# Gate projections of the DeltaNet branch between the branch products of the merge, and sums of the middle branches on VectorE alone

## The chip, the cores and the metric

One core of a Trainium2 chip runs the whole program in one launch. The core has five engines that run side by side, each with its own instruction stream in a fixed order: TensorE (PE, matrix products, with its weight loads shown as PEld), VectorE (DVE), ScalarE (ACT), GpSimd (POOL) and SyncE (SP, which here only issues DMAs). They wait for each other by semaphores. The metric is the time of one execution in microseconds of device time, as the median of several runs; less is better.

## The reference

The program computes one layer of a streaming encoder for two groups of tokens (1024 prompt tokens and 64 sample tokens with a cache of 256; 1088 columns in all), in float32, with width 1024. What matters here is the mixing step:

```
proj = u @ w_in                                  # u = rms_norm(x), 1088 x 1024
fox, dif, sb, gdn, gates = split(proj)           # gates: 4 branches x 1024 columns
o_fox  = softmax attention with a forget bias    # 4 heads of 64, causal
o_diff = rms_norm(softmax(q1 k1) v - lam * softmax(q2 k2) v)   # chunk-causal
o_sb   = stick-breaking attention                # strictly causal
o_gdn  = gated DeltaNet: short convolution, chunks of 64, a recurrence over chunks
gate   = sigmoid(gates)                          # per branch, 1088 x 1024
merged = sum over b of gate[b] * (o_b @ w_branch[b])           # o_b is 1088 x 256
x = x + merged @ w_out
x = x + (silu(h @ wg) * (h @ wu)) @ wd           # h = rms_norm(x)
y = rms_norm(x)
```

The caches' new rows, the DeltaNet state and the convolution state are outputs too.

## The kernel before, in words

**Numbers.** Each float32 operand of a large product is split into two float16 parts, high and low, and a product is three matmuls into one PSUM bank: high x high, high x low, low x high. `gemm_a` (lines 176 to 187) does that with the weights as the stationary operand: for each of `K` blocks of 128 rows it issues three matmuls with up to 364 columns. A split of weights is one ScalarE copy with scale (`acopy`, line 61) and one VectorE instruction that takes the remainder (`stt`, line 64); `load_unit` does it for a unit of 1024 x 256 weights, in two halves of 512 KB.

**Gate projections.** `spill_gates(b, sp)` is a generator that computes the gate logits of one branch: 4 units of weights, each 2 x 128 output rows x 3 pieces of 364, 364 and 360 columns, 24 groups in all. A group is 24 matmuls (8 blocks x 3) into one of two PSUM banks of tag `d`, a ScalarE copy into a tile `ths` of two buffers, and a store to DRAM (`gtd[b]`) issued from GpSimd's queue; then it yields. The four generators are put on the list `dense` before the forgetting attention begins, in the order sb, fox, diff, gdn.

**Order of the work.** A scheduler at build time simulates the engines and puts each engine's instructions into a fixed order: an instruction written earlier goes first if it is ready, and one written later may go ahead of it into a hole. Three things steer it. `fill(us)` inside the attention loops takes groups from `dense` until their stated costs (3.7 each) use up the given allowance, which sets where they stand in the written order. `tc.high_priority()` lets loads and evacuations of PSUM go ahead. `tc.issue_after(ins)` forbids the instructions traced inside it to go ahead of `ins` on its engine. What `fill` leaves is run off by `drain(dense)` after `attend_diff`, as written; the scheduler may pull it ahead.

**Attention.** `attend_diff` runs over 2 pairs of heads; in each over the nine query tiles in the order `QORD` = 7, 6, 5, 4, 3, 2, 8, 1, 0 (tile t has (t+1) x 128 keys, tile 8 has 320); in each over 2 heads and 2 halves of a head. For each half `scores` puts the scores into PSUM (tag `s`, three banks), VectorE takes the maximum (line 644), ScalarE the exponential with its sum (line 653); then VectorE combines the halves, ScalarE and VectorE split the result, a transposing DMA turns it, and `diff_out` multiplies with the values.

**Merge.** After the attention a loop runs over the branches in the order sb, fox, diff, gdn (`bi` 0 to 3). It loads and splits the branch's weights (`wb`, tiles `wbh`, `wbl`), loads its outputs `oT`, and makes 24 branch products: 8 blocks of 128 output rows (`d`) x 3 pieces. For each: load the gate logits back (`thg`, line 1137), ScalarE tanh, 6 matmuls into a bank `ptb` taken in turn from the five banks of tags `s` and `g`, one VectorE instruction (1 + tanh) x product, and for all but the first branch an addition to the running sum `mg[d]`. In fox and diff this addition is on VectorE for the third piece and on GpSimd otherwise; in gdn on VectorE for `d % 3 == 2` and on GpSimd otherwise. In gdn the sum is then split into `mT`, the input of the product with `w_out`. `mT` takes the buffer of `u1`, the input of the gate projections, so it can be written only when the last of these is done. Tiles of `th` have 4 buffers in the sb branch and 12 after. Sums `mg0` to `mg2` and the sb branch's `th` lie in the pool `brp`, which is open before `attend_diff` ends; the others in one that opens after it.

`load_out(c)` loads and splits one of four units of `w_out`. It takes its tiles from `wt`, which hands out two slots of the ordinary weight pool and, once `w3` is open, every third time a slot of that pool; `w3` opens after the attention's pool has closed. Units 1 and 2 are loaded in the fox branch, 3 and 0 in the diff branch. The products with `w_out` (`out_tile`, `out_sample`) may not go ahead of the last branch product (`last_ptb`). The second half of the layer follows.

Of the kernel before, what the change touches and what calls it, by code (L numbers as in the profile page):

```python
# [17 lines left out]
P = 128  # L18
# [35 lines left out]
def tile_hybrid_encoder(ctx, tc, i, o):  # L54
# [397 lines left out]
    def scores(ps, n, w, q0, q1, kk, col, mask, diag):  # L452

        two = q1 is not None
        last = mask is None and not two
        pe.matmul(ps[:n, :w], lhsT=q0, rhs=kk[:, col:col + w], start=True, stop=last)
        if mask is not None:
            pe.matmul(ps[:n, diag:diag + n], lhsT=identb[:n, :n], rhs=mask[:n, :n], start=False, stop=not two)
        if two:
            pe.matmul(ps[:n, :w], lhsT=q1, rhs=kk[:, col:col + w], start=False, stop=True)  # L460

    def pv_pair(b, pair, t, n, vt, vl, pts):
        ps = pso("pv")
# [161 lines left out]
    def attend_diff():  # L625
        for pair in range(2):
            kT, vt = load_kv("diff", pair)
            for t in QORD:
                n, kc, W, vl = qgeom(t)
                nb = len(vl)  # L630
                o32 = at.tile([P, 2, 64], F32, tag="o32", name="o32", bufs=3)
                qt = load_q("diff", pair, t, n)
                for hp in range(2):
                    sm = at.tile([P, 16], F32, tag="sm16", name="sm16", bufs=4)
                    pr = []
                    ch = chunks(W)
                    for c in range(2):
                        p = at.tile([P, 1024], F32, tag="wk", name="p", bufs=6)
                        pss = []
                        for cc, (c0, w) in enumerate(ch):  # L640
                            ps = psc()
                            m = mk_diff if (t < 8 and c0 + w == W) else None
                            scores(ps, n, w, qt[:, 2 * hp + c, :n], None, kT[2 * hp + c], kc + c0, m, W - n - c0)
                            vec.tensor_reduce(out=sm[:n, 2 * c + cc:2 * c + cc + 1], in_=ps[:n, :w], op=ALU.max, axis=AX.X)
                            pss.append(ps)
                        nm = sm[:n, 4 + c:5 + c]
                        if len(ch) == 2:
                            tt(nm, sm[:n, 2 * c:2 * c + 1], sm[:n, 2 * c + 1:2 * c + 2], ALU.max)
                            ts(nm, nm, -SC, None, ALU.mult)
                        else:  # L650
                            ts(nm, sm[:n, 2 * c:2 * c + 1], -SC, None, ALU.mult)
                        for cc, (c0, w) in enumerate(ch):
                            act.activation(p[:n, c0:c0 + w], pss[cc][:n, :w], AF.Exp, scale=SC, bias=nm,
                                           accum_out=sm[:n, 6 + 2 * c + cc:7 + 2 * c + cc])
                        if len(ch) == 2:
                            tt(sm[:n, 10 + c:11 + c], sm[:n, 6 + 2 * c:7 + 2 * c], sm[:n, 7 + 2 * c:8 + 2 * c], ALU.add)
                            l = 10 + c
                        else:
                            l = 6 + 2 * c
                        pr.append((p, sm[:n, l:l + 1]))  # L660
                    (p1, l1), (p2, l2) = pr
                    cf, r1 = sm[:n, 12:13], sm[:n, 13:14]
                    vec.reciprocal(cf, l2)
                    stt(cf, cf, l1, nlam[:n], ALU.mult, ALU.mult)
                    vec.reciprocal(r1, l1)
                    ts(r1, r1, PS, None, ALU.mult)
                    stt(p1[:n, :W], p2[:n, :W], cf, p1[:n, :W], ALU.mult, ALU.add)
                    sv, tr = p_tiles(W, n)
                    acopy(sv[:n, 0, :W], p1[:n, :W], r1)
                    stt(sv[:n, 1, :W], p1[:n, :W], r1, sv[:n, 0, :W], ALU.mult, ALU.subtract)  # L670
                    pt = tr()
                    fill(FILL_DIFF * W / 2)
                    diff_out(pair, t, n, nb, vl, vt, hp, pt, o32)
# [360 lines left out]

    bidx = {"fox": 0, "diff": 1, "sb": 2, "gdn": 3}

    def spill_gates(b, sp):
        j = bidx[b]
        for d2 in range(4):
            wu = load_unit([(w_in, 0, OFF_GATE + j * D + d2 * BW, BW)], BW)  # L1040
            for m in range(2):
                d = 2 * d2 + m
                for off, n in PIECES:
                    pg = pd("pgs")
                    gemm_a(pg, wu, m * P, uh, ul, off, n, KD)
                    th = sp.tile([P, 364], F32, tag="ths", name="ths", bufs=2)
                    with tc.high_priority():
                        acopy(th[:, :n], pg[:, :n], 0.5 * IWS)
                    gps.dma_start(gtd[b][d * P:(d + 1) * P, off:off + n], th[:, :n])
                    yield 3.7  # L1050
# [28 lines left out]
    cb = cb_.enter_context(tc.tile_pool(name="cb", bufs=1, side="right", reuse_waits="tile"))  # L1079
    gd_ = ExitStack()  # L1080
    g3 = gd_.enter_context(tc.tile_pool(name="gp3", bufs=1, side="right", reuse_waits="tile"))
    dense += [spill_gates(b, sp) for b in gtd]
    side.append(gdn_seq(g3))
    attend_fox()
    drain(side)
# [5 lines left out]
    drain(dense)  # L1091
    ap_.close()
    gp_ = ExitStack()
    mT = up.tile([P, 2, KD, T], F16, tag="u", name="mT")
    w3p = ctx.enter_context(tc.tile_pool(name="w3", bufs=1, reuse_waits="tile"))
    w3.append(w3p)
    w_out = i["w_out"][0]
# [13 lines left out]
    nb_ = [0]  # L1111
    mg = [(brp if d < 3 else gt_pool).tile([P, T], F32, tag=f"mg{d}", name=f"mg{d}") for d in range(KD)]
    order = ("sb", "fox", "diff", "gdn")
    for bi, b in enumerate(order):
        j = bidx[b]
        oT = brp.tile([P, 2, 2, T], F16, tag="oT", name="oT", bufs=2)
        if b in ("sb", "fox"):
            for pr in range(2):
# [9 lines left out]
            acopy(wbh[:, k], wv, WS)  # L1128
            stt(wbl[:, k], wv, WS, wbh[:, k], ALU.mult, ALU.subtract)
        last = bi == len(order) - 1  # L1130
        for c in {1: (1, 2), 2: (3, 0)}.get(bi, ()):
            load_out(c)
        for d, (off, n) in [(d, PIECES[p]) for p in (0, 2, 1) for d in range(KD)] if last else \
                [(d, p) for d in range(KD) for p in PIECES]:
# [3 lines left out]
            act.activation(th[:, :n], th[:, :n], AF.Tanh)  # L1138
            pt = pbk[nb_[0] % len(pbk)]("ptb")
            nb_[0] += 1  # L1140
            last_ptb = gemm_a(pt, (wbh, wbl), d * P, oT[:, 0], oT[:, 1], off, n, 2)
            if bi == 0:
                stt(mg[d][:, off:off + n], th[:, :n], 1.0, pt[:, :n], ALU.add, ALU.mult)
            else:
                stt(th[:, :n], th[:, :n], 1.0, pt[:, :n], ALU.add, ALU.mult)
                tt(mg[d][:, off:off + n], mg[d][:, off:off + n], th[:, :n], ALU.add,
                   eng=vec if (d % 3 == 2 if last else off >= 728) else gps)
            if last:
                sl = slice(off, off + n)
                acopy(mT[:, 0, d, sl], mg[d][:, sl], 0.5 * IWS)  # L1150
# [62 lines left out]
    def out_tile(t, c, wu):  # L1213
        n = rows(t)
        ps = pob[nb_[0] % len(pob)]("pout")
        nb_[0] += 1
        with tc.issue_after(last_ptb.ins):
            gemm_b(ps, n, mT[:, 0], mT[:, 1], t * P, wu, BW)
        cs = slice(c * BW, (c + 1) * BW)
        stt(x2[t][:n, cs], ps[:n, :BW], IWS, x2[t][:n, cs], ALU.mult, ALU.add)  # L1220
# [6 lines left out]
    def out_sample():  # L1227

        for (ca, wa_), (cb2, wb_) in (wus[0:2], wus[2:4]):
            ps = pob[nb_[0] % len(pob)]("pout")  # L1230
            nb_[0] += 1
            with tc.issue_after(last_ptb.ins):
                gemm_2(ps, SMP, mT[:, 0], mT[:, 1], 8 * P, wa_, wb_, BW)
            for r, c in ((slice(0, SMP), ca), (slice(SMP, P), cb2)):
                cs = slice(c * BW, (c + 1) * BW)
# [267 lines left out]
```

## Time and profile before

| what | value |
| --- | --- |
| time of three runs | 1860.31 us median (1857.23 to 1861.63) |
| the profiled execution's own time | 1859.53 us |
| its span, first to last instruction | 1857.4 us |
| TensorE busy | 1730.3 us, 93% |
| VectorE busy | 1252.1 us, 67% |
| ScalarE busy | 863.9 us, 47% |
| GpSimd busy | 301.2 us, 16% |
| TensorE's mean granted clock | 0.981 of full speed |

Times inside the program are microseconds from the start of the span. Busy shares count overlapping instructions of an engine once; a matmul is shown longer than the distance to the next one, because matmuls are pipelined, so the pace is read from the starts. A clock of 1.00 means 2.4 GHz; the other level is 1.2 GHz, and a value between is a mean over time. The releaser of an idle time is inferred from semaphores. The first output of the forgetting attention is stored at 546 us, the first of the differential attention at 699 and its last at 979; the last matmul of a branch product starts at 1077.8 us.

### The profile page before, as it was taken

How to read it: one execution, taken by the hardware profiler on the slowest of the kernel's cores; microseconds unless marked ns; L12 is line 12 of the kernel's file. 1: busy time of each engine (PE TensorE's matmuls, PEld its weight loads, DVE VectorE, ACT ScalarE, POOL GpSimd, SP SyncE). 2: the span in 40 equal slices, each digit the busy share in tenths (PEclk: the TensorE clock that was granted, in tenths of full speed). 3: DMA queues.
4: the chain of work that ended last, by engine and by line, in shares of the span. 5: the costliest groups of instructions: out<-in, count | busy, mean ns of one | idle time of the engine just before them, and what ended most of it. 6: DMA issues, size and time to landing. Idle time of an engine off the chain costs nothing.

```text
span 1857.4 us, 36710 instructions
## 1 busy us (share of the span) xinstructions
PE 1730.3 (93%) x14364; PEld 1226.1 (66%) x14364; DVE 1252.1 (67%) x2589; ACT 863.9 (47%) x1819; POOL 301.2 (16%) x445
## 2 busy tenths in 40 slices
PE   7999983898989899999998899999999999999997
PEld 5678873675655566666665578777758668577573
DVE  7558872997775677786766886758537456465465
ACT  6336551887764555565555533423314223133132
POOL 2114231002212122232133630000000000000002
PEclk9999997999998999999999999999999999999999
DMA  6267798889998975656759846412211113112113
GB/s 225 49 106 212 205 226 137 196 200 213 197 186 202 192 173 141 151 139 172 188 110 283 231 137 109 101 52 69 69 35 58 46 46 91 35 35 69 35 46 102
DMA packets 412158, 244.61 MB, mean 132 GB/s; under 512 B 266146, under 2 KB 389502, under 8 KB 411916
## 3 DMA queue, kind: packets, MB, share of 16 engines
q1 hardware_dynamic: 398944, 205.67, 46.3%
q0 software_dynamic: 13040, 36.60, 7.3%
q8 instruction: 112, 1.84, 0.4%
q14 instruction: 62, 0.51, 0.1%
HBM read 123.39 MB, written 60.81 MB: 99 GB/s over the span
## 4 chain that ended last, share of the span: by engine, by line
PE 42%; DVE 5%; DMA 4%; issue 1%; ACT 1%; POOL 1%; SPq 0%; DVEq 0%; POOLq 0%; ACTq 0%
PE po L1425 12%; PE pb L1309 3%; PE pb L1308 3%; PE pb L1310 3%; PE pc L1309 2%; PE pc L1310 2%; PE pa L1310 2%; PE pc L1308 2%; PE pa L1309 2%; PE pa L1308 2%; PE pout L165 1%; PE pout L166 1%; PE pout L167 1%; PE pgs L184 1%; PE pgs L185 1%
## 5 line engine op out<-in xcount | busy, mean ns | idle before, releaser
L183 PE MATMUL pgs<-u,wh 128*128 128x364 f16 (+1 forms) x768 | 246.3, 321 | 0.0
L185 PE MATMUL pgs<-u,wl 128*128 128x364 f16 (+1 forms) x768 | 246.3, 321 | 0.0
L184 PE MATMUL pgs<-u,wh 128*128 128x364 f16 (+1 forms) x768 | 246.1, 320 | 0.0
L1425 PE MATMUL po<-wh,hT 128*128 128x512 f16 (+1 forms) x792 | 238.1, 380 | 0.6 <-DVE x2a L64 0.6
L1425 PEld LDWEIGHTS <-hT 128*128 128x128 f16 (+1 forms) x1188 | 109.2, 99 | 120.0 <-issue 7.6
L64 DVE SCALAR_TENSOR_TENSOR x2a<-po,x2a 128x512 f32<-128x512 f32 x108 | 74.4, 689 | 140.4 <-PE po L1425 140.2
L61 ACT ACTIVATE wh<-w32f 128x1024 f16<-128x1024 f32 (+1 forms) x90 | 80.3, 926 | 160.2 <-PE po L1425 111.7
L165 PE MATMUL pd<-wh,u 128*128 128x256 f16 (+1 forms) x456 | 126.7, 278 | 29.7 <-DVE qs L64 29.0
L1308 PE MATMUL pb<-X,wh 128*128 128x288 f16 (+1 forms) x528 | 147.1, 279 | 2.5 <-DMA X<-nsh 2.2
L64 DVE SCALAR_TENSOR_TENSOR wl<-w32f,wh 128x1024 f16<-128x1024 f32 (+1 forms) x90 | 94.7, 1065 | 79.5 <-ACT wh L61 79.5
L1309 PE MATMUL pb<-X,wh 128*128 128x288 f16 (+1 forms) x528 | 147.2, 279 | 0.2 <-DMA X<-nsl 0.2
L1310 PE MATMUL pb<-X,wl 128*128 128x256 f16 (+1 forms) x528 | 146.3, 279 | 0.0
L1425 PE MATMUL po<-wl,hT 128*128 128x512 f16 (+1 forms) x396 | 142.0, 379 | 0.0
L1308 PEld LDWEIGHTS <-wh 128*128 128x128 f16 x1232 | 120.5, 98 | 31.0 <-issue 2.4
L1309 PEld LDWEIGHTS <-wh 128*128 128x128 f16 x1232 | 120.5, 98 | 29.9 <-issue 2.4
L1310 PEld LDWEIGHTS <-wl 128*128 128x128 f16 x1232 | 120.5, 98 | 27.2 <-issue 0.8
L166 PE MATMUL pd<-wl,u 128*128 128x256 f16 (+1 forms) x456 | 126.5, 277 | 0.0
L167 PE MATMUL pd<-wh,u 128*128 128x256 f16 (+1 forms) x456 | 126.4, 277 | 0.0
L185 PEld LDWEIGHTS <-wl 128*128 128x128 f16 x912 | 90.0, 99 | 50.9 <-issue 1.5
L183 PEld LDWEIGHTS <-wh 128*128 128x128 f16 x912 | 89.9, 99 | 50.5 <-issue 1.2
L184 PEld LDWEIGHTS <-wh 128*128 128x128 f16 x912 | 89.9, 99 | 49.7 <-issue 0.6
L71 POOL TENSOR_SCALAR fss<-fss 128x1 f32<-128x1 f32 (+1 forms) x9 | 2.0, 220 | 660.3 <-ACT fsq L1454 660.3
(393 smaller groups left out, 4624.6 us busy)
## 6 DMA issues: line engine op xcount, KB each, us to landing
w<-in_w_in_dram SPq DMA_DIRECT2D x56, 512.0 KB, 5.2
w32f<-in_w_ffn_gate_dram SPq DMA_DIRECT2D x20, 512.0 KB, 4.9
w32f<-in_w_ffn_up_dram SPq DMA_DIRECT2D x20, 512.0 KB, 4.0
w32f<-in_w_ffn_down_dram SPq DMA_DIRECT2D x20, 512.0 KB, 3.6
xt<-in_x_prompt_dram SPq DMA_DIRECT2D x8, 512.0 KB, 7.1
wb<-in_w_branch_dram SPq DMA_DIRECT2D x8, 512.0 KB, 4.1
w<-in_w_out_dram SPq DMA_DIRECT2D x8, 512.0 KB, 5.8
x2a<-in_x_prompt_dram SPq DMA_DIRECT2D x8, 512.0 KB, 7.3
```

The source lines that it names most:

```text
L61: return act.activation(out, in_, AF.Copy, scale=scale)
L64: return vec.scalar_tensor_tensor(out=out, in0=in0, scalar=s, in1=in1, op0=op0, op1=op1)
L165: pe.matmul(ps[:n, :N], lhsT=a, rhs=wh[:, k, :N], start=(k == 0), stop=False)
L166: pe.matmul(ps[:n, :N], lhsT=a, rhs=wl[:, k, :N], start=False, stop=False)
L167: pe.matmul(ps[:n, :N], lhsT=b, rhs=wh[:, k, :N], start=False, stop=(k == K - 1))
L183: pe.matmul(ps[:, :n], lhsT=a, rhs=xh[:, k, off:off + n], start=(k == 0), stop=False)
L184: pe.matmul(ps[:, :n], lhsT=a, rhs=xl[:, k, off:off + n], start=False, stop=False)
L185: mm = pe.matmul(ps[:, :n], lhsT=b, rhs=xh[:, k, off:off + n], start=False, stop=(k == K - 1))
L1308: pe.matmul(ps[:, :n], lhsT=wh[:, k], rhs=xh_, start=(start and k == 0), stop=False, skip_group_check=not start)
L1309: pe.matmul(ps[:, :n], lhsT=wh[:, k], rhs=xl_, start=False, stop=False, skip_group_check=not start)
L1310: mm = pe.matmul(ps[:, :n], lhsT=wl[:, k], rhs=xh_, start=False, stop=(k == 3), skip_group_check=not start)
L1425: pe.matmul(ps[h * n:h * n + n], lhsT=hts[k + h][:, a, tk:tk + n], rhs=w[:, k + h], start=(k == 0 and a == 0 and w is wh), stop=(k + nh >= ...
```

## The change

Four things, all in the same place of the program:

1. gdn's gate generator is no longer on `dense`. It is named `late`, and the merge loop asks it for one group after every second branch product of the sb, fox and diff branches (until its 24 groups are used up), and for what is left before the gdn branch. Each group's matmuls may not go ahead of `gate_mark`, which is the last score matmul of pair 1, tile t=3, in `attend_diff`.
2. `mT` is allocated when the generator is done.
3. The additions of the fox and diff branches are all on VectorE. Those of the gdn branch stay as they were.
4. `load_out` of units 1 and 2 moves from the fox to the diff branch, that of 3 and 0 from the diff to the gdn branch.

```diff
@@ -453,11 +453,12 @@
 
         two = q1 is not None
         last = mask is None and not two
-        pe.matmul(ps[:n, :w], lhsT=q0, rhs=kk[:, col:col + w], start=True, stop=last)
+        mm = pe.matmul(ps[:n, :w], lhsT=q0, rhs=kk[:, col:col + w], start=True, stop=last)
         if mask is not None:
             pe.matmul(ps[:n, diag:diag + n], lhsT=identb[:n, :n], rhs=mask[:n, :n], start=False, stop=not two)
         if two:
             pe.matmul(ps[:n, :w], lhsT=q1, rhs=kk[:, col:col + w], start=False, stop=True)
+        return mm
 
     def pv_pair(b, pair, t, n, vt, vl, pts):
         ps = pso("pv")
@@ -640,7 +641,9 @@
                         for cc, (c0, w) in enumerate(ch):
                             ps = psc()
                             m = mk_diff if (t < 8 and c0 + w == W) else None
-                            scores(ps, n, w, qt[:, 2 * hp + c, :n], None, kT[2 * hp + c], kc + c0, m, W - n - c0)
+                            mm = scores(ps, n, w, qt[:, 2 * hp + c, :n], None, kT[2 * hp + c], kc + c0, m, W - n - c0)
+                            if pair == 1 and t == 3:
+                                gate_mark[0] = mm
                             vec.tensor_reduce(out=sm[:n, 2 * c + cc:2 * c + cc + 1], in_=ps[:n, :w], op=ALU.max, axis=AX.X)
                             pss.append(ps)
                         nm = sm[:n, 4 + c:5 + c]
@@ -1034,6 +1037,8 @@
 
     bidx = {"fox": 0, "diff": 1, "sb": 2, "gdn": 3}
 
+    gate_mark = [None]
+
     def spill_gates(b, sp):
         j = bidx[b]
         for d2 in range(4):
@@ -1042,7 +1047,8 @@
                 d = 2 * d2 + m
                 for off, n in PIECES:
                     pg = pd("pgs")
-                    gemm_a(pg, wu, m * P, uh, ul, off, n, KD)
+                    with tc.issue_after(gate_mark[0].ins) if b == "gdn" else ExitStack():
+                        gemm_a(pg, wu, m * P, uh, ul, off, n, KD)
                     th = sp.tile([P, 364], F32, tag="ths", name="ths", bufs=2)
                     with tc.high_priority():
                         acopy(th[:, :n], pg[:, :n], 0.5 * IWS)
@@ -1079,7 +1085,7 @@
     cb = cb_.enter_context(tc.tile_pool(name="cb", bufs=1, side="right", reuse_waits="tile"))
     gd_ = ExitStack()
     g3 = gd_.enter_context(tc.tile_pool(name="gp3", bufs=1, side="right", reuse_waits="tile"))
-    dense += [spill_gates(b, sp) for b in gtd]
+    dense += [spill_gates(b, sp) for b in ("sb", "fox", "diff")]
     side.append(gdn_seq(g3))
     attend_fox()
     drain(side)
@@ -1091,7 +1097,6 @@
     drain(dense)
     ap_.close()
     gp_ = ExitStack()
-    mT = up.tile([P, 2, KD, T], F16, tag="u", name="mT")
     w3p = ctx.enter_context(tc.tile_pool(name="w3", bufs=1, reuse_waits="tile"))
     w3.append(w3p)
     w_out = i["w_out"][0]
@@ -1111,8 +1116,14 @@
     nb_ = [0]
     mg = [(brp if d < 3 else gt_pool).tile([P, T], F32, tag=f"mg{d}", name=f"mg{d}") for d in range(KD)]
     order = ("sb", "fox", "diff", "gdn")
+    late = spill_gates("gdn", sp)
+    ptb = []
     for bi, b in enumerate(order):
         j = bidx[b]
+        if bi == len(order) - 1:
+            for _ in late:
+                pass
+            mT = up.tile([P, 2, KD, T], F16, tag="u", name="mT")
         oT = brp.tile([P, 2, 2, T], F16, tag="oT", name="oT", bufs=2)
         if b in ("sb", "fox"):
             for pr in range(2):
@@ -1128,7 +1139,7 @@
             acopy(wbh[:, k], wv, WS)
             stt(wbl[:, k], wv, WS, wbh[:, k], ALU.mult, ALU.subtract)
         last = bi == len(order) - 1
-        for c in {1: (1, 2), 2: (3, 0)}.get(bi, ()):
+        for c in {2: (1, 2), 3: (3, 0)}.get(bi, ()):
             load_out(c)
         for d, (off, n) in [(d, PIECES[p]) for p in (0, 2, 1) for d in range(KD)] if last else \
                 [(d, p) for d in range(KD) for p in PIECES]:
@@ -1138,13 +1149,15 @@
             act.activation(th[:, :n], th[:, :n], AF.Tanh)
             pt = pbk[nb_[0] % len(pbk)]("ptb")
             nb_[0] += 1
-            last_ptb = gemm_a(pt, (wbh, wbl), d * P, oT[:, 0], oT[:, 1], off, n, 2)
+            ptb.append(gemm_a(pt, (wbh, wbl), d * P, oT[:, 0], oT[:, 1], off, n, 2))
+            if len(ptb) % 2 == 0 and not last:
+                next(late, None)
             if bi == 0:
                 stt(mg[d][:, off:off + n], th[:, :n], 1.0, pt[:, :n], ALU.add, ALU.mult)
             else:
                 stt(th[:, :n], th[:, :n], 1.0, pt[:, :n], ALU.add, ALU.mult)
                 tt(mg[d][:, off:off + n], mg[d][:, off:off + n], th[:, :n], ALU.add,
-                   eng=vec if (d % 3 == 2 if last else off >= 728) else gps)
+                   eng=gps if last and d % 3 != 2 else vec)
             if last:
                 sl = slice(off, off + n)
                 acopy(mT[:, 0, d, sl], mg[d][:, sl], 0.5 * IWS)
@@ -1214,7 +1227,7 @@
         n = rows(t)
         ps = pob[nb_[0] % len(pob)]("pout")
         nb_[0] += 1
-        with tc.issue_after(last_ptb.ins):
+        with tc.issue_after(ptb[-1].ins):
             gemm_b(ps, n, mT[:, 0], mT[:, 1], t * P, wu, BW)
         cs = slice(c * BW, (c + 1) * BW)
         stt(x2[t][:n, cs], ps[:n, :BW], IWS, x2[t][:n, cs], ALU.mult, ALU.add)
@@ -1229,7 +1242,7 @@
         for (ca, wa_), (cb2, wb_) in (wus[0:2], wus[2:4]):
             ps = pob[nb_[0] % len(pob)]("pout")
             nb_[0] += 1
-            with tc.issue_after(last_ptb.ins):
+            with tc.issue_after(ptb[-1].ins):
                 gemm_2(ps, SMP, mT[:, 0], mT[:, 1], 8 * P, wa_, wb_, BW)
             for r, c in ((slice(0, SMP), ca), (slice(SMP, P), cb2)):
                 cs = slice(c * BW, (c + 1) * BW)
```

## Rows read from the trace of the kernel before

**Rows 1.** The page, part 1: busy us (share of the span) xinstructions.

```profile
PE 1730.3 (93%) x14364; PEld 1226.1 (66%) x14364; DVE 1252.1 (67%) x2589; ACT 863.9 (47%) x1819; POOL 301.2 (16%) x445
```

**Rows 2.** Busy time by stretch; after the engines: granted clock, DMA share, GB/s.

```profile
864.00:916.00 52.00, 50.47 (x372) 32.51 (x370) 31.90 (x90) 29.16 (x71) 15.26 (x26) 1.00 0.80 212
916.00:970.00 54.00, 52.62 (x388) 33.70 (x387) 37.77 (x138) 30.06 (x88) 15.08 (x27) 1.00 0.60 142
970.00:1000.00 30.00, 25.70 (x154) 15.25 (x153) 18.43 (x33) 19.80 (x39) 4.71 (x6) 0.94 0.80 240
1000.00:1022.00 22.00, 19.52 (x125) 12.17 (x125) 17.32 (x33) 9.66 (x19) 14.14 (x13) 1.00 0.94 287
1022.00:1046.00 24.00, 20.77 (x132) 12.62 (x131) 22.10 (x33) 12.90 (x26) 17.94 (x19) 1.00 1.05 298
1046.00:1079.00 33.00, 25.94 (x173) 15.79 (x173) 29.37 (x48) 18.97 (x41) 20.40 (x19) 1.00 0.45 134
```

**Rows 3.** Waits of TensorE, 970 to 1079 us: total us, times, longest.

```profile
PE ptb L183 <- DVE thg L64: 13.7, 15, 2.0
PE ptb L183 <- DVE mg L64: 3.3, 4, 2.0
```

**Rows 4.** Tiles gtd_diff, gtd_gdn: ns min/median/max, first and last start us.

```profile
L1049 POOL DMA_DIRECT2D gtd_diff<-ths x24: 539/556/623, 742.3 to 864.6; - x24
...
L1049 POOL DMA_DIRECT2D gtd_gdn<-ths x24: 539/556/626, 868.0 to 973.1; - x24
L1137 SPq DMA_DIRECT2D thg<-gtd_gdn x24: 319/320/1073, 1041.9 to 1068.3; - x24
```

**Rows 5.** Timeline of TensorE at the marked score: start us, duration us.

```profile
916.27 0.38 PE L456 MATMUL psc<-kT,qt 128*128 128x512 f16 x1
```

**Rows 6.** Busy time by stretch, instructions of tile pgs alone.

```profile
864.00:916.00 52.00, 47.01 (x289) 5.36 (x12) 1.00 0.80 212
916.00:970.00 54.00, 46.10 (x280) 5.59 (x12) 1.00 0.60 142
```

**Rows 7.** Timeline of TensorE, gate matmuls and the first sb product.

```profile
902.77 0.32 PE L184 MATMUL pgs<-u,wh 128*128 128x364 f16 x1
...
904.00 0.32 PE L183 MATMUL ptb<-oT,wbh 128*128 128x364 f16 x1
```

**Rows 8.** VectorE by form, 864 to 916: busy us, mean ns, idle before.

```profile
L64 DVE SCALAR_TENSOR_TENSOR wl<-w,wh 128x1024 f16<-128x1024 f32 x4 | 4.8, 1219 | 0.0
L64 DVE SCALAR_TENSOR_TENSOR wbl<-wb,wbh 128x1024 f16<-128x1024 f32 x3 | 3.7, 1226 | 4.8 <-ACT wbh L61 4.8
L67 DVE TENSOR_TENSOR sm<-sm 128x1 f32<-128x1 f32 x16 | 2.5, 154 | 6.9 <-ACT p L653 6.8
```

**Rows 9.** Busy time by stretch, instructions of tile ptb alone.

```profile
864.00:916.00 52.00, 0.63 (x3) 0.00 (x0) 1.00 0.80 212
916.00:970.00 54.00, 3.21 (x18) 1.03 (x2) 1.00 0.60 142
```

**Rows 10.** Tile mg: ns min/median/max, first and last start us.

```profile
L67 DVE TENSOR_TENSOR mg<-mg,thg x22: 519/532/3069, 1002.1 to 1083.3; 128x360 f32<-128x360 f32 x18, 128x364 f32<-128x364 f32 x4
```

**Rows 11.** VectorE by form, 970 to 1079.

```profile
L67 DVE TENSOR_TENSOR mg<-mg,thg 128x360 f32<-128x360 f32 x18 | 16.1, 898 | 0.3
```

**Rows 12.** Timeline of VectorE in the fox branch.

```profile
1002.06 0.52 DVE L67 TENSOR_TENSOR mg<-mg,thg 128x360 f32<-128x360 f32 x1
1002.50 0.52 DVE L64 SCALAR_TENSOR_TENSOR thg<-thg,ptb 128x364 f32<-128x364 f32 x1
```

**Rows 13.** Timeline of the diff branch, VectorE and GpSimd.

```profile
1030.49 4.59 POOL L67 TENSOR_TENSOR mg<-mg,thg 128x364 f32<-128x364 f32 x5
...
1032.42 3.07 DVE L67 TENSOR_TENSOR mg<-mg,thg 128x360 f32<-128x360 f32 x1
```

**Rows 14.** Timeline of TensorE after a wait.

```profile
980.90 0.51 PE L184 MATMUL ptb<-oT,wbh 128*128 128x364 f16 x1
981.20 0.51 PE L185 MATMUL ptb<-oT,wbl 128*128 128x364 f16 x1
```

## Prediction

> **What bounds the kernel now.** I read the busy shares first, then the engines by stretch, then the gate projections by stretch, then the waits of TensorE. [rows 1] shows TensorE busy 93% of the span and VectorE 67%; the program is bound by the order of work on TensorE, and a gain can only come out of TensorE's idle time. [rows 2] shows where that is around the change. From 864 to 970 us TensorE is nearly full: 1.5 and 1.4 us are idle in the first two stretches. In the merge it is not: 4.3 us (970 to 1000, mostly the sb branch), 2.5 us (1000 to 1022, fox), 3.2 us (1022 to 1046, diff), 7.1 us (1046 to 1079, gdn), together 17.1 us. [rows 3] names what ends these waits: in all 19 of them, 17.0 us, a branch product waits for VectorE to empty a PSUM bank.
>
> [rows 4] says what keeps TensorE full before the merge. Gate projections are pulled ahead of their place in the program into every hole of the attention: the last gate tile that is not gdn's leaves for DRAM at 864.6 us, gdn's from 868.0 to 973.1. The tile that `gate_mark` names (pair 1, t=3, last score) runs at 916.3 us [rows 5]. So gdn's gates now begin 52 us ahead of the mark, inside the differential attention. [rows 6] counts them: 289 gate matmuls between 864 and 916, or 12 of gdn's 24 groups, and 280 more up to 970.
>
> **Part 1: gdn's gates may not run before the mark.** The first 72 groups (sb, fox, diff) keep their order, priority and weights, so I take everything up to 864 as unchanged. After that TensorE has no gate work until the mark. Gate matmuls follow each other 0.154 us apart ([rows 7]: eight steps from 902.77 to 904.00), so what leaves the stretch 864 to 916 is 289 x 0.154 = 44.5 us. Of its 50.5 us of TensorE work 6.0 us stay: scores and value products of four tiles.
>
> How short does that stretch get? It cannot shrink to 6 us, for the attention also needs VectorE and ScalarE, which were hidden beside the gates. VectorE works 31.9 us in it [rows 2]. Of this the splits of gate and branch weights take 4.8 + 3.7 us [rows 8], which could run at another time; without them 23.4 us are left, and that is the lower bound. The upper bound is the 52 us of now, if the chain from score to maximum to exponential to sum sets the pace whatever TensorE does; [rows 8] shows VectorE idle 6.8 us there for ScalarE's exponentials. I take 31.9 us: VectorE without a pause, nearest to the row of the same work. TensorE is then idle 31.9 - 6.0 = 25.9 us less what else it finds to do. That is branch products of sb, which come later in the program but are free to come early. The first starts at 904.0 [rows 7], and only 21 of their matmuls (3.5 products) run before 970 [rows 9], because a product needs one of four early gate buffers and VectorE to empty it. At 0.154 us these 21 are 3.2 us; the bounds are none and the 9 products whose sum buffers exist that early (54 x 0.154 = 8.3 us). I take 3.2 us. **New idle time: 22.7 us**, between 23.4 - 6.0 - 8.3 = 9 and 52 - 6 = 46 us.
>
> **Part 2: the merge gets gates to fill its holes.** After the mark, 24 groups are to be placed where there were 12. The tail of the attention up to 970 took 12 groups and was full, and it will take about as many again: weights for two of the four units (12 groups) fit the two slots of the ordinary pool, and the third unit sits in the pool that opens when the attention's buffers close. So about 12 groups (44 us) fall between the sb and fox products, whose waits (4.3 + 2.5 us) they cover. The request for a group stands after every second product, 24 groups after 48 products, so the diff branch gets none by program order; of its 3.2 us I count half as gained, for the reason in part 3. The gdn branch keeps its 7.1 us: no gates are left. Gain 8.4 us, between 0 and 17.1. The groups' other instructions move with them: 24 ScalarE copies (about 0.45 us each, [rows 6]), 24 stores from GpSimd's queue, 8 weight loads on SyncE's queue and 8 splits on each of ScalarE and VectorE. ScalarE is busy 19.8 us of 30 in sb and 9.7 of 22 in fox [rows 2], and these stretches become twice as long, so the copies are covered; uncovered they would be 12 x 0.45 = 5.4 us.
>
> The gdn gates are stored later and read back in the gdn branch. Now the last store is issued at 973 and the first load at 1041.9 [rows 4]. In the new order a diff branch of about 24 us lies between, and a load lands in a few us, so I cost this at nothing; without that cover it would be one landing, some 4 us, at the head of the last branch.
>
> **Part 3: sums of fox and diff on VectorE alone.** 32 additions leave GpSimd (0.92 us each there, [rows 13]: five in 4.59) and come to VectorE [rows 10]. There they need not cost 0.9 us, the mean of those that VectorE makes now [rows 11]: that mean hides a spread from 0.52 us, which is also the median (0.53), to 3.07 us [rows 10], and the long one, at 1032.4, lies beside that chain of five on GpSimd. Starts back to back are 0.45 us apart [rows 12]. A product then costs VectorE 2 x 0.45 = 0.9 us against 6 x 0.154 = 0.92 us on TensorE, and a branch 24 x 0.9 + 2 weight splits of 1.2 = 24 us against 22.2. That is the 24 us that the diff stretch takes now, so nothing is lost and perhaps 1.6 us gained. The bound on the bad side is the present mean: 24 x (0.45 + 0.9) = 32 us, or +8 for diff; on the good side 3.2 us. The Trainium skill says in "SBUF — State Buffer", section "Who interferes with whom", that a VectorE instruction with two SBUF inputs and a GpSimd one block each other wholly, not by shares. The 3.07 us row agrees, and by that rule the move alone would free VectorE rather than load it, which makes it the support of the faster rival below.
>
> **Part 4: `load_out` one branch later.** Two of the four w_out units (4 VectorE splits of 1.22 us, the mean of [rows 8], 4.9 us) now belong to the gdn branch, where VectorE has 33 - 29.4 = 3.6 us free [rows 2]. Cost 4.9 - 3.6 = 1.3 us; between 0, if they run early beside gates, and 4.9. The two units in the diff branch have gates' time ahead of them and cost nothing if hoisted there, 4.9 us if not.
>
> **Clock.** After the 2.0 us wait at 978 to 980 the granted clock fell to 1.2 GHz for a few us (the mean over 970 to 1000 is 0.94, [rows 2]) and twelve matmuls ran 0.30 us apart instead of 0.154 [rows 14], 1.8 us lost. A gap before the mark will bring the same once, at the first gates; the present fall should go, as gates stand in that wait. Net zero; bound +4 if the gap makes it fall twice. The Trainium skill's "TensorE: Matmul & The Clock Gate", section "What's actually happening", says that the throttled state is the default and activity releases it. By it, a thin TensorE load through the new gap leaves the first gates at the lower level, which is the 1.8 us just named.
>
> **Sum.** +22.7 - 8.4 + 1.3 = +15.6 us. The profiled execution took 1859.5 us (span 1857.4 and 2.1 around it); with the sum 1875.1. The median of the runs shown is 0.8 us above it, so I predict 1876 us.
>
> **Rivals.**
> *Faster: the gap is short and the whole merge fills.* The attention up to the mark needs only the 23.4 us of VectorE, nine sb products move into it (9 us idle), and VectorE, freed of GpSimd, ends all 17.1 us of merge waits: 9 - 17 = -8 us, 1852 us. For it: the 3.07 us row. Against it: [rows 9] show just 3.5 products early, and the gdn branch keeps its sums on GpSimd. It decides where the idle time ahead of the mark falls under what the merge gives back, 8 to 17 us. Chance 0.20.
> *No change:* idle time ahead of the mark within 4 us of what the merge gives back, 1857 to 1864 us. Chance 0.09.
> *Much slower:* the chain of the attention does not tighten (38 us idle, with VectorE's pauses of [rows 8] kept: 38 - 8.4 + 1.3 = +31), or the sums and the w_out splits make diff and gdn VectorE-bound at +8 and +5 (15.6 + 13 = +29): about 1890 us. For it: the DMA share of 0.94 to 1.05 in fox and diff [rows 2], into which loads move. Chance 0.11.
> *The forecast,* a gap that outweighs the filled waits, 1864 to 1887 us: 0.60.
>
> **How the numbers follow.** A measurement of this kernel cannot tell less than about 0.2% (3.7 us) from no change. Faster 0.20, same 0.09, slower 0.60 + 0.11 = 0.71. The likeliest case alone has 1864 to 1887. The range takes in the much slower case and the faster one down to its worked time: 1852 to 1893.
>
> **What would show it.** Right: in the changed trace the last diff gate leaves near 864, then TensorE's busy share falls to about a third for some 30 us, no gdn gate starts before the last t=3 score, and the waits of branch products for VectorE vanish in sb and fox but stay in gdn. Wrong: TensorE full between the last diff gate and the mark (other work was pulled in), or gates spread so that the diff attention is no shorter, or a gdn branch with no waits. VectorE's additions near 0.5 us would confirm part 3.

## The result, and the profile after

The changed kernel takes 1872.3 us (median of 6 runs, 1866.4 to 1878.9), the kernel before 1859.5 us on the same chip. The ratio is 1.0070, with a 95% interval of 1.0053 to 1.0087: slower by 10 to 16 us. The profiled execution took 1872.8 us (span 1871.1).

The page, part 1 of the changed kernel (compare [rows 1]):

```profile
PE 1739.0 (93%) x14364; PEld 1231.2 (66%) x14364; DVE 1256.2 (67%) x2621; ACT 863.9 (46%) x1819; POOL 267.2 (14%) x413
```

GpSimd has 32 instructions fewer and VectorE 32 more: the additions. TensorE makes the same 14364 matmuls but is busy 8.7 us longer; some of them ran at the lower clock, and some stand alone, where a matmul counts with its shown length (0.32 us in [rows 7]) and not with the step to the next (0.154).

The gate stores of the last two branches (compare [rows 4]), and the marked score on TensorE with the first gdn gate behind it ([rows 5], [rows 14]); start, duration:

```profile
L1055 POOL DMA_DIRECT2D gtd_diff<-ths x24: 539/556/623, 738.6 to 862.0; - x24
...
L1055 POOL DMA_DIRECT2D gtd_gdn<-ths x24: 540/550/637, 904.6 to 1036.9; - x24
L1148 SPq DMA_DIRECT2D thg<-gtd_gdn x24: 319/320/895, 1056.1 to 1078.6; - x24
```

```profile
896.19 0.61 PE L456 MATMUL psc<-kT,qt 128*128 128x512 f16 x1
896.60 0.31 PE L458 MATMUL psc<-mk_diff,identb 128*128 128x128 bf16 x1
896.71 0.51 PE L183 MATMUL pgs<-u,wh 128*128 128x364 f16 x1
897.01 0.51 PE L184 MATMUL pgs<-u,wh 128*128 128x364 f16 x1
...
899.43 0.50 PE L183 MATMUL pgs<-u,wh 128*128 128x364 f16 x1
899.74 0.34 PE L184 MATMUL pgs<-u,wh 128*128 128x364 f16 x1
899.92 0.32 PE L185 MATMUL pgs<-u,wl 128*128 128x364 f16 x1
```

The last diff gate leaves at 862.0 and the first gdn gate runs at 896.7, right behind the mark: 34.7 us without gates. The last gdn gate is stored 19 us before its branch reads the first one, so that hand-over holds up no branch product.

Busy time by stretch after (us, TensorE, weight loads, VectorE, ScalarE, GpSimd, then granted clock, DMA share and GB/s; compare [rows 2]): the gap, the tail of the attention, sb with fox, diff, gdn.

```profile
862.00:896.70 34.70, 16.06 (x90) 8.96 (x90) 29.54 (x89) 22.98 (x55) 9.18 (x12) 0.65 0.86 235
896.70:957.00 60.30, 59.84 (x433) 37.94 (x432) 37.98 (x145) 31.92 (x97) 16.32 (x31) 0.97 0.49 128
957.00:1040.00 83.00, 83.00 (x543) 52.83 (x541) 46.51 (x81) 37.40 (x71) 8.30 (x15) 1.00 0.72 212
1040.00:1062.00 22.00, 19.76 (x127) 12.23 (x126) 19.82 (x41) 11.42 (x21) 2.70 (x3) 1.00 0.94 289
1062.00:1090.00 28.00, 23.30 (x173) 14.79 (x172) 28.00 (x49) 17.75 (x40) 18.71 (x16) 1.00 0.52 150
```

The same for tile ptb in the gap (TensorE, VectorE; compare [rows 9]), then for tile pgs in the gap, in the tail and in sb with fox (TensorE, ScalarE; compare [rows 6]):

```profile
862.00:896.70 34.70, 6.00 (x24) 1.07 (x2) 0.65 0.86 235
```

```profile
862.00:896.70 34.70, 0.00 (x0) 0.00 (x0) 0.65 0.86 235
896.70:957.00 60.30, 46.25 (x271) 5.10 (x11) 0.97 0.49 128
957.00:1040.00 83.00, 49.47 (x307) 5.96 (x13) 1.00 0.72 212
```

Waits of TensorE in the gap, then (second fence) from there to the last branch product (total us, times, longest; compare [rows 3]):

```profile
PE psc L456 <- ACT p L656: 13.4, 6, 4.4
PE ptb L183 <- DMA oT<-od_sb: 3.0, 1, 3.0
PE po L603 <- DMA pt<-st: 2.1, 1, 2.1
```

```profile
PE ptb L183 <- DVE thg L64: 6.8, 7, 1.7
PE ptb L183 <- DVE mg L64: 0.5, 1, 0.5
```

The merge is as it was meant to be: not one idle microsecond in sb and fox, 7.3 us of waits where there were 17.0. The gap costs more than that. In it TensorE waits mostly for ScalarE: a new score needs one of three PSUM banks, and a bank is free only when the exponential has read it. VectorE is busy 29.5 of the 34.7 us, so by these rows it sets the pace nearly as much.

Both sides of the account, with the end of the merge as the clock. From the last diff gate's store to the last matmul of a branch product was 864.6 to 1077.8 before, 213.2 us; now it is 862.0 to 1087.5, 225.5 us: +12.3. The span is 13.7 longer: the changed profile is 2.6 us early at the first of these points, and behind the second it takes 4.0 us more (783.6 against 779.6). What made these two differences is open; each is of the size by which executions of one kernel differ here. The interval of 10 to 16 us holds both sums.

### The profile page after: what moved, and what is told of

It is laid out like the page before. It is cut to its first block, busy times and chain, and to the rows that moved or that the text cites. A ratio compares the mean times of both kernels' runs of the same rounds, so it can differ in the third digit from the quotient of the medians.

```text
span 1871.1 us, 36684 instructions
## 1 busy us (share of the span) xinstructions
PE 1739.0 (93%) x14364; PEld 1231.2 (66%) x14364; DVE 1256.2 (67%) x2621; ACT 863.9 (46%) x1819; POOL 267.2 (14%) x413
## 4 chain that ended last, share of the span: by engine, by line
PE 65%; DVE 12%; DMA 11%; issue 5%; ACT 4%; POOL 1%; SPq 1%; DVEq 0%; POOLq 0%; ACTq 0%
PE po L1438 12%; PE pgs L184 4%; PE pgs L185 4%; PE pgs L183 4%; DMA pt<-st 4%; PE pb L1321 3%; PE pb L1323 3%; PE pb L1322 3%; PE pa L1323 2%; PE pc L1322 2%; PE pa L1322 2%; PE pa L1321 2%; PE pc L1323 2%; PE pc L1321 2%; DMA gt<-stg 1%
## 5 line engine op out<-in xcount | busy, mean ns | idle before, releaser
L1321 PE MATMUL pa<-X,wh 128*128 128x256 f16 (+1 forms) x352 | 98.4, 281 | 1.7 <-ACT wh L61 1.1
```

The costliest lines, as they stand in the source:

```text
L1321: pe.matmul(ps[:, :n], lhsT=wh[:, k], rhs=xh_, start=(start and k == 0), stop=False, skip_group_check=not start)
```

## The experiments

Each was run in five rounds beside the kernel before; ratios are to that kernel, with the 95% interval. The gap theory says that the loss is the hole in the attention, because gdn's gates are kept out of it. The merge theory says that the loss is in the merge: the additions on VectorE, or `load_out` one branch later. The first four runs, and the kernel with neither hindrance further down, separate them.

**No mark.** The changed kernel, gates free to go ahead of the mark.

```diff
-                    with tc.issue_after(gate_mark[0].ins) if b == "gdn" else ExitStack():
+                    with ExitStack():
```

> The change without the rule that gdn's gates may not go ahead of the marked score; all else as changed. Gap theory (the 13 us are TensorE's idle time ahead of the mark, less what the merge gives back): gates start again near 862 us. If the mark alone held them back, the hole of 18.6 us closes and the ratio to before is 0.995 to 0.999. If weight slots hold back the third and fourth unit (they are free only when the attention's pool closes), 12 groups fill the first hole and a hole of 10 to 20 us opens in the tail of the attention, 916 to 960: ratio 1.001 to 1.006. Merge theory (the time is lost in the merge, by VectorE's sums and the later w_out splits): no change against the changed kernel, 1.006 to 1.008.

Measured 1875.2 us, 1.0081 [1.0060, 1.0102]: no gain at all. By the number alone the merge theory would have it, and the gap theory's 1.001 to 1.006 is missed. The trace decides otherwise. Busy time by stretch of all instructions, then of the gate matmuls alone:

```profile
900.00:920.00 20.00, 18.80 (x141) 12.15 (x142) 11.48 (x37) 9.33 (x26) 4.37 (x7) 1.00 0.41 114
920.00:940.00 20.00, 9.52 (x70) 5.61 (x69) 18.04 (x85) 14.46 (x47) 3.39 (x6) 0.65 0.43 87
940.00:960.00 20.00, 14.00 (x86) 8.21 (x86) 12.37 (x50) 9.33 (x34) 6.60 (x12) 0.76 0.45 120
```

```profile
860.00:925.00 65.00, 49.97 (x304) 6.03 (x13) 1.00 0.66 195
925.00:965.00 40.00, 0.78 (x4) 0.00 (x0) 0.66 0.46 114
965.00:1045.00 80.00, 45.75 (x284) 5.46 (x12) 1.00 0.72 207
```

The gates now begin at once, but only 304 matmuls run between 860 and 925. The first 16 end diff's last group; the other 288 are two of gdn's four units (2 x 6 groups x 24). Then there are no gates for 43 us, and a hole like the first opens some 60 us later (921 to 964 instead of 862 to 897), at the same clock of 0.65 in its deepest stretch. The change moved the generator behind the opening of pool `w3`, and `wt` gives every third unit a slot there; that memory is the attention's until the attention ends. So there may be two hindrances, of which the mark is one; the runs with the ordinary pool below test it.

**The sums alone**, in the kernel before.

```diff
-                   eng=vec if (d % 3 == 2 if last else off >= 728) else gps)
+                   eng=gps if last and d % 3 != 2 else vec)
```

> The kernel before with only the sums of fox and diff moved to VectorE. Gap theory: 0.998 to 1.000, since VectorE's additions cost 0.45 us apart without GpSimd beside them and TensorE's waits in fox and diff (5.7 us) shrink or stay. Merge theory: 1.003 or more, VectorE's 32 additions show up as longer waits of the branch products in fox and diff.

Measured 1859.0 us, 0.9995 [0.9978, 1.0012]. The sums alone do not make the loss.

**The gates alone:** the changed kernel with the sums shared as before (the same lines, exchanged).

> The changed kernel with the sums of fox and diff shared with GpSimd as before. Gap theory: the hole is the same 18 us, and the sums are covered by gates in fox and nearly covered in diff: 1.006 to 1.009, equal to the changed kernel within the interval. Merge theory: clearly less than the changed kernel's, 1.000 to 1.004, since VectorE is relieved.

Measured 1877.4 us, 1.0103 [1.0081, 1.0125], above the 1.006 to 1.009 of the gap theory. The hole is there (TensorE is busy 7.6 of the 20 us from 860 to 880, at a clock of 0.59), and the merge's waits are 11.2 us. Beside the changed kernel's 1.0070 and 6.8 us of the same wait, the additions on VectorE may be a small help rather than a cost; the two intervals overlap, so that is not shown.

**`load_out` alone**, in the kernel before.

```diff
-        for c in {1: (1, 2), 2: (3, 0)}.get(bi, ()):
+        for c in {2: (1, 2), 3: (3, 0)}.get(bi, ()):
```

> The kernel before with load_out one branch later and nothing else. Gap theory: 0 to 5 us in the gdn branch, 1.000 to 1.002. Merge theory: 1.003 or more.

Measured 1859.3 us, 0.9998 [0.9981, 1.0015]: nothing. Neither cause of the merge theory makes the loss alone. Both are in the kernel below that is free of the loss, so together they do not make it either.

**The dose.** Only the last 12, 6 or 3 of gdn's groups come late. The others stand on `dense` as before; the late ones are tied to every 4th, 8th or 16th branch product instead of the mark (other parts as changed).

```diff
-    dense += [spill_gates(b, sp) for b in ("sb", "fox", "diff")]
+    late = spill_gates("gdn", sp)
+    dense += [spill_gates(b, sp) for b in ("sb", "fox", "diff")] + [islice(late, 12)]
...
-            if len(ptb) % 2 == 0 and not last:
+            if len(ptb) % 4 == 0 and not last:
+                gate_mark[0] = ptb[-1]
                 next(late, None)
```

> The changed kernel, but the first 12 of gdn's 24 groups go back on the list of the attention and only the last 12 go into the merge, one after every fourth product and each not ahead of that product; no mark. Gap theory: the hole at 862 is filled (12 groups, 44 us), the tail of the attention from 916 lacks its 12 groups and leaves TensorE idle for 10 to 20 us, the merge's waits fall from 17 to about 7 us: 1.000 to 1.005. Merge theory: 1.005 to 1.008, as the merge is the changed kernel's.

> As the one with 12 late groups, but 18 groups go back to the attention and 6 into the merge, one after every eighth product. Gap theory: the attention misses only 6 groups (22 us) at its very end, of which it loses 5 to 8 us as idle time, and the merge gives back 7 to 10 us: 0.996 to 1.001. Merge theory: 1.004 to 1.008.

> As the ones with 12 and 6 late groups, but only 3 groups in the merge, one after every sixteenth product. Gap theory: a late group costs about 0.5 us net (12 gave +5.9 us, 6 gave +3.0), so 1.000 to 1.002; faster than before, down to 0.998, only if the first groups that go to the merge meet its waits in full (3 x 3.7 = 11 us of 17) while the attention's end loses less than that. Merge theory: 1.004 or more, as sums and w_out splits are the changed kernel's.

Measured: 12 late 1863.6 us, 1.0030 [1.0012, 1.0048]; 6 late 1860.7 us, 1.0014 [0.9997, 1.0030]; 3 late 1856.2 us, 0.9998 [0.9982, 1.0014]. With 24 late it was 1.0070. The last two cannot be told from no change, and 6 late lies above the 0.996 to 1.001 that was expected. Each has a hole, smaller and nearer the end of the attention as the dose falls (with 6 late it is in two parts, 900 to 920 and 960 to 980). The deepest stretch with 12 late, then with 3:

```profile
920.00:940.00 20.00, 11.45 (x78) 6.41 (x75) 19.59 (x81) 13.43 (x43) 4.25 (x7) 0.68 0.71 156
```

```profile
960.00:980.00 20.00, 13.77 (x78) 7.99 (x76) 8.63 (x25) 7.71 (x21) 3.84 (x7) 0.75 0.48 145
```

So with 24 and 12 late a group costs the attention more than it gives the merge, some 0.5 us net each (13 us / 24, 5.6 / 12); the 2.6 us with 6 late would fit but are within the noise.

**Both hindrances away, and each alone.** gdn's gate weights go into the ordinary pool: a flag that `wt` asks, set around `load_unit` in `spill_gates`. First without the mark, then with it.

```diff
-        if w3:
+        if w3 and not plain[0]:
...
+            plain[0] = b == "gdn"
             wu = load_unit([(w_in, 0, OFF_GATE + j * D + d2 * BW, BW)], BW)
+            plain[0] = False
```

> The changed kernel without the mark, and with all four units of gdn's gate weights in the two slots of the ordinary pool, so that the third unit need not wait for the pool that opens after the attention. Gap theory, with slots as the second thing that holds gates back: all 24 groups are pulled ahead into the attention as in the kernel before, no hole at 862 nor at 920, last gate leaves for DRAM at 970 to 985, the merge waits 14 to 17 us again: ratio 0.997 to 1.002. Merge theory (written order in the merge, sums and w_out splits cost the time): 1.005 or more.

> The changed kernel with the mark, and all four units of gdn's gate weights in the ordinary pool's two slots: the fourth corner beside the changed kernel (mark, pool of the merge), the one without the mark, and the one without either. Gap theory: the mark alone makes the hole of about 18 us before it, so nothing is gained there; after it 24 groups can be pulled into the attention's tail: 1.004 to 1.008. If the pool of the merge were the only cause, it would fall to 0.998 to 1.000.

| ratio | weights may lie in `w3` | ordinary pool |
| --- | --- | --- |
| with the mark | 1.0070 [1.0053, 1.0087] (the change) | 1.0068 [1.0047, 1.0090] |
| without | 1.0081 [1.0060, 1.0102] | 0.9977 [0.9962, 0.9992] |

Only the fourth cell is free of the loss. The first fence shows 860 to 900 with the mark and the ordinary pool, the second 860 to 960 of the kernel with neither hindrance:

```profile
860.00:880.00 20.00, 10.27 (x104) 6.42 (x102) 13.55 (x38) 10.25 (x24) 4.49 (x6) 0.85 0.52 115
880.00:900.00 20.00, 9.63 (x51) 5.00 (x51) 17.07 (x47) 14.29 (x34) 5.26 (x7) 0.67 1.11 312
```

```profile
860.00:880.00 20.00, 20.00 (x147) 12.96 (x144) 13.44 (x30) 13.12 (x28) 8.38 (x12) 1.00 0.87 273
880.00:900.00 20.00, 19.41 (x143) 12.24 (x142) 14.99 (x41) 12.56 (x32) 5.81 (x9) 1.00 0.95 262
900.00:920.00 20.00, 20.00 (x151) 13.05 (x150) 13.96 (x41) 11.83 (x30) 3.77 (x7) 1.00 0.46 87
920.00:940.00 20.00, 20.00 (x147) 12.57 (x145) 16.04 (x68) 11.49 (x39) 6.08 (x11) 1.00 0.70 171
940.00:960.00 20.00, 19.33 (x146) 12.34 (x144) 13.49 (x49) 10.86 (x32) 4.32 (x8) 1.00 0.59 159
```

No hole is left, and this kernel is faster than the one before (1852.8 us). All of gdn's gates run ahead of 976 us in it, as in the kernel before, so the merge has no gates to fill its waits with: they are 15.9 us, against 17.0. One of them is 7.7 us long, in the diff branch, behind a `w_out` split that waits for its load.

**A better version.** Two attempts to be rid of that long wait, both with neither hindrance. One asks for a gate group after every product and puts `load_out` back; the other puts all of `load_out` into the diff branch.

```diff
-        for c in {2: (1, 2), 3: (3, 0)}.get(bi, ()):
+        for c in {1: (1, 2), 2: (3, 0)}.get(bi, ()):
...
-            if len(ptb) % 2 == 0 and not last:
+            if not last:
```

> The kernel without mark and with gdn's weights in the ordinary pool (ratio 0.9977), gates asked for after every product instead of every second, and load_out back to the fox and diff branches as before. In that kernel's trace TensorE waits 7.7 us at 1023 to 1031 us, behind ScalarE's split of the last w_out half, whose load was issued at 1018.3. If the earlier request brings it in time, that wait goes and the ratio is 0.993 to 0.996; if the load only collides with the gates' loads of the fox branch, 0.997 to 0.999.

Measured 1858.1 us, 0.9995 [0.9979, 1.0012]. The merge's waits are 15.8 us, and the gain is gone; both ranges of the expectation are missed.

```diff
-        for c in {2: (1, 2), 3: (3, 0)}.get(bi, ()):
+        for c in {2: (1, 2, 3, 0)}.get(bi, ()):
```

> The kernel without mark and with gdn's weights in the ordinary pool, with all four units of w_out requested at the head of the diff branch. Same question about the 7.7 us wait: 0.993 to 0.996 if the load of the last unit is then early enough, 0.997 to 0.999 if it makes another wait of the same size.

Measured 1852.2 us, 0.9961 [0.9946, 0.9976]: faster than the kernel before and the changed one, but not clearly than the 0.9977 above, and so short of the 0.993 to 0.996 expected for a wait that goes. Its waits of TensorE for VectorE in the merge:

```profile
PE ptb L184 <- DVE thg L64: 9.6, 12, 2.9
PE ptb L184 <- DVE mg L64: 2.8, 3, 1.5
```

**What carries that gain.** The same kernel with the additions shared with GpSimd as before.

> The kernel of the run before last of this study that beat both (0.9961 of the time before: no mark, gdn's gate weights in the ordinary pool, all four w_out units in the diff branch), but with the additions of fox and diff shared with GpSimd as before. What is left of the change is the written order: gdn's gates stand in the merge, behind sb products. If the written order alone carries that gain (sb products pulled into the attention's tail, gates in the merge's first branch), the ratio stays at 0.994 to 0.998, with the sum of TensorE's waits for VectorE in the merge near 9 to 13 us. If the gain needs VectorE's additions as well (moving the sums was worth 0.003 inside the changed kernel), the ratio is 0.998 to 1.001 and the waits are 15 us or more.

Measured 1852.5 us, 0.9964 [0.9939, 0.9990], with 12.1 us of waits for VectorE in the merge: the gain needs no sums on VectorE. What remains in it is the written order (gdn's gates behind the sb products, with `mT` allocated after them) and the place of `load_out`. Branch products by stretch (TensorE, VectorE), first in the kernel before, then in this one:

```profile
940.00:960.00 20.00, 1.66 (x9) 0.00 (x0) 1.00 0.64 142
960.00:980.00 20.00, 8.24 (x51) 2.46 (x5) 1.00 0.43 136
```

```profile
940.00:960.00 20.00, 10.35 (x60) 3.59 (x7) 1.00 0.66 189
960.00:980.00 20.00, 5.04 (x33) 4.15 (x9) 1.00 0.54 178
```

All instructions, from 860 to 970 and from 970 to 1070, in the same order of kernels:

```profile
860.00:970.00 110.00, 107.08 (x810) 69.07 (x808) 72.56 (x232) 62.15 (x164) 30.34 (x53) 1.00 0.68 170
970.00:1070.00 100.00, 84.84 (x525) 51.49 (x524) 78.23 (x129) 57.64 (x115) 51.34 (x49) 0.98 0.83 244
```

```profile
860.00:970.00 110.00, 109.15 (x794) 69.75 (x792) 75.17 (x240) 63.29 (x167) 32.84 (x55) 1.00 0.68 183
970.00:1070.00 100.00, 87.64 (x558) 53.67 (x558) 81.30 (x131) 57.20 (x114) 58.60 (x53) 0.97 0.80 238
```

As the sb products are now written ahead of the gates, 60 of their matmuls run between 940 and 960 instead of 9, and gates are left over for the stretch behind. TensorE is busy 196.8 of the 210 us, against 191.9 before: 4.9 us, most of the 6.3 us between the medians. Only 2.1 of the 4.9 lie ahead of 970. The kernel with neither hindrance has 60 early matmuls too, and still waits 15.9 us in the merge where this one waits 12.1, so the other 2.8 us may belong to the place of `load_out`. No run took the order or that place alone: what carries the gain is open.

## Why the prediction was right

The time lies in the range, 4 us under the forecast, and the mechanism is the forecast's: a gap ahead of the mark that outweighs the waits filled in the merge. Most of the 4 us is the merge, which gave back 11.1 us where 8.4 - 1.3 = 7.1 were forecast. Its terms beside what the trace of the changed kernel gives:

| term | predicted | measured |
| --- | --- | --- |
| TensorE time lost ahead of the mark (estimate below) | +22.7 | +23.5 |
| attention tail and merge filled | -8.4 | -11.1 with `load_out` |
| `load_out` later | +1.3 | in the line above |
| clock after the gap | 0 | -0.3 |
| sum | +15.6 | +12.1 (+12.3 from end to end) |

*The gap.* It is 34.7 us long against 31.9 forecast, and holds four early sb products (24 matmuls) against three and a half. By the prediction's own figure for the scores and value products the work in it is worth 6.0 + 24 x 0.154 = 9.7 us at the full clock, so 25.0 us are lost; 1.5 of these were idle before [rows 2], which the prediction did not take off. This is an estimate, at the low end: the 6.0 us hold three sb matmuls and 80 of scores and values, the gap only 66 of these, and in that proportion 26.4 us are lost. The sum of the table is then 13.5 instead of 12.1, with 12.3 measured between them. That 22.7 and 23.5 lie so close is partly luck: the gap came out 2.8 us longer than forecast, and the 1.5 us left out go the other way. TensorE's idle time in it is 18.6 us and not 22.7; the rest of the loss is slow work, which the forecast put at nothing. VectorE's busy time was the right end to choose, for a reason in part wrong: VectorE is busy 29.5 us without the pauses of [rows 8] (0.2 us of the 6.8 are left), but TensorE waits 13.4 us for the exponentials that free the score banks. By these waits the chain through all three engines sets the pace, not VectorE alone; no run took it apart. TensorE shows 16.1 us busy, not 9.7, in part because the granted clock was 0.65 (12 of the 24 sb matmuls follow each other 0.30 us apart, the other 12 at 0.15), in part because a matmul that stands alone is shown longer. Idle time alone (18.6 us) would therefore understate the loss. The sign named in advance, TensorE busy for a third of some 30 us, came out as 46% of 34.7 us.

*The merge.* That the tail takes about 12 groups again and about 12 fall between the sb and fox products came out: 271 and 307 gate matmuls, 11 and 13 groups. Idle time from the mark's old or new place to the end of the merge went from 18.5 us (1.4 + 17.1, [rows 2]) to 7.4 (0.5 + 0 + 2.2 + 4.7). The half of diff's 3.2 us counted as gained was too much, 2.2 stay; the gdn branch, costed at its old 7.1 us and 1.3 more, lost less than before.

*The sums.* They cost VectorE what the median said and not the mean. VectorE's additions after, and GpSimd's in gdn (ns min/median/max, first and last start; compare [rows 10]):

```profile
L67 DVE TENSOR_TENSOR mg<-mg,thg x54: 521/534/1283, 976.9 to 1093.0; 128x364 f32<-128x364 f32 x36, 128x360 f32<-128x360 f32 x18
...
L67 POOL TENSOR_TENSOR mg<-mg,thg x18: 946/1240/1372, 1064.2 to 1092.6; 128x364 f32<-128x364 f32 x12, 128x360 f32<-128x360 f32 x6
```

The addition of 3.07 us [rows 13] has gone with the GpSimd chain beside it: the longest is now 1.28 us. The page "SBUF — State Buffer" of the Trainium skill, section "Who interferes with whom", has the two engines block each other in such operations, and the 3.07 us beside the chain agrees. Yet the rival that built on this gave it the whole merge: freed of the chains, diff still waits 2.2 us, and the sums alone in the kernel before gave 0.9995.

*The clock.* Ten gate matmuls behind the gap take steps of 0.30 us (896.71 to 899.74), 1.5 us lost, and the old fall at 981 [rows 14], 1.8 us, is gone. This is the cancelling pair that was forecast; the slow matmuls inside the gap were not.

*Where it was blind.* The prediction saw that the third unit's slot lies in the pool that opens late, and used it only to place the groups behind the mark. It is a second hindrance: either one alone costs as much as both (1.0081 and 1.0068 beside 1.0070). A forecast for the change without the mark would have gone wrong there: with free gates it would have called the gap closed, and 1.0081 was measured. It also took everything up to 864 us as unchanged; the changed profile is 2.6 us early there.

## What to carry to other kernels

Work that fills holes is worth what it fills: before moving it into a later hole, work out how short the stretch it leaves can get without it, from the other engines' chain there; 17 us of waits in the merge, of which 9.7 went away, were no reason to lose some 25 us in the attention. What could be pulled ahead here was bounded by the weight buffers as well as by the order, so a constraint taken away alone may change nothing (1.0081) and two together everything (0.9977). The kernel that gained has its fillers written behind the work that they should fill around, with the scheduler free to pull both; which part of it gave the gain is not settled.

## What was not expected of the hardware

A gap with thin TensorE work is dearer than its idle time: over 34.7 us with 16.1 us busy the granted clock was 0.65, which as a mean of the two levels puts some 70% of it at the lower one of 1.2 GHz, and half of the sb matmuls that were pulled in to use the gap took twice their time (12 of 24 were 0.30 us apart instead of 0.154):

```profile
879.25 0.51 PE L185 MATMUL ptb<-oT,wbl 128*128 128x364 f16 x1
879.55 0.51 PE L183 MATMUL ptb<-oT,wbh 128*128 128x364 f16 x1
```

In the hole of the kernel without the mark it was 0.65 again, with 9.5 of 20 us busy. The Trainium skill's "TensorE: Matmul & The Clock Gate", section "What's actually happening", has the throttled state as the default that activity lifts, which these stretches agree with.
